# Two layers of a hybrid encoder on one core: banks and order of the output projection's first group, the place where linear attention is closed, and two elementwise operations on GpSimd

## The chip, the cores and the metric

The kernel runs on one core of a Trainium2 chip. A core has five engines with queues of their own, each working strictly in order: TensorE (PE) multiplies matrices into PSUM, VectorE (DVE) and ScalarE (ACT) do elementwise work and read PSUM, GpSimd (POOL) does elementwise work in SBUF, and SyncE (SP) issues most of the transfers. Engines wait for each other by semaphores. The accumulators live in PSUM banks of 128 partitions x 512 float32.

The metric is the device time of one execution in microseconds (us). A profile is one further execution with the hardware profiler on.

## The reference

Everything is float32. Two layers run over 256 tokens with 16 learned meta tokens in front (272 columns in all), model width 2048:

```python
proj = h @ w_in        # columns: GLA q k v gate, low-rank decay, NA q k v
y_gla = gla(...)       # bidirectional gated linear attention, 4 heads
y_na  = na(...)        # 16 heads of 2-D neighbourhood attention + meta keys
mix = concat(y_gla, y_na) @ w_out
h = layer_norm(alpha * h + mix)
h = layer_norm(alpha * h + square(relu(h @ w_ff1)) @ w_ff2)
```

The linear attention of a head ends in a norm over its 256 values and a gate:

```python
o = o * rsqrt(mean(square(o), axis=-1) + eps) * norm_w   # per head
o = o * silu(r)
```

The neighbourhood attention is a softmax of each token's scores over its window and the meta tokens; the 16 meta tokens attend among themselves, a softmax of 16 x 16 per head (kept here in a 16 x 48 tile with a mask). The meta rows are dropped from the result, so layer 1 computes the mixer's output and what follows for the 256 tokens only (n = 256; in layer 0 n = 272).

## The kernel before, in words

Activations stand transposed, features on the partitions and tokens along a row. A weight block is 128 x 1024 float32 (`raw`, loaded by SP at L195). Each block, and each activation, is split into a rounded high part and the remainder: `wh` by ScalarE (L218), `wl` by VectorE (L219). A product is then three passes (high by high, high by low, low by high), 24 matmuls of 272 columns for a block. Blocks are made two ahead, from buffers of three, so a `wl` that comes late stops TensorE.

Outputs are computed in groups of four. `by_m` goes output by output (L253, in layer 1 partly L265): an accumulator is finished over all of k before the next. `by_k` (L304, in layer 1 L314 by `dense`) holds four accumulators and goes through k in pairs; it is used where the activations become ready one by one, as for the first group of the output projection, whose inputs `y` come out of the two kinds of attention: `y[0..7]` from linear attention, `y[8..15]` from neighbourhood attention. Ahead of each k pair it calls `mixed`, which makes sure that this pair of `y` is done and adds up the residual (`acc`, L424).

PSUM has eight banks in two pools of four: `pm` (tiles `mm`: accumulators, and in this stage the scores of neighbourhood attention) and `pb` (tiles `bg`, handed out by `bank()`: everything else in the background). A bank is reused when its last reader is done.

Two queues of generators run in the background of the projections: `bg` holds the heads of linear attention one after another, `fg` the eight pairs of heads of neighbourhood attention (`na_pair`, pairs 0 to 7). `pump` lets them go on by a credit in the middle and at the end of each output. The 24 q/k/v outputs of neighbourhood attention are six groups (g = 0 to 5); pair c can begin when output 3c + 2 is there, so pair 6 begins after the first output of group 5, and pair 7 after the last. What is left of `bg` is forced ahead of group 5.

The program order of each engine's queue comes from a scheduler that follows the order of the code but may move an instruction by its own model.

The end of a head of linear attention: squares of the outputs (`grs`, `gtn`), their sum (L725), the split of the sum into `sp` (ScalarE L339, VectorE L340), two matmuls with a matrix of 1/256 that give the mean (L983), the inverse root by Newton steps (L574 to L578) and the scaling that gives two `y`.

The end of a neighbourhood pair: scores on TensorE (L778, for the meta tokens L782), bias added by VectorE (L787 to `ns`, L789 to `nms`), maximum (L754), exponentials on ScalarE (L756), reciprocals of the sums (L757), products (L760; for `ns` and its rest `npr` on GpSimd, for the meta rows `nms` on VectorE), then transposes: those of `ns` and `npr` on VectorE (L799, L800), those of the values and of `nms` on TensorE (L805 to L808). A trip through memory (`hop` to `np`) puts the turned weights in place for the products with the values (L851, L858). The values and keys of a pair stand in `nv` and `nk`, with their neighbours' columns in `nr` (L540, L541, L544).

Of the kernel before, what the change touches and what calls it, by code (L numbers as in the profile page):

```python
# [7 lines left out]
F32 = mybir.dt.float32  # L8
# [3 lines left out]
ALU = mybir.AluOpType  # L12
PSUM = bass.MemoryType.PSUM

P = 128
# [19 lines left out]
GLA_R, GLA_NA, NORMS = 1.3, 1.4, (1.0, 0.6)  # L35
# [23 lines left out]
class Trunk:  # L59
# [216 lines left out]
        self.nc.vector.tensor_tensor(t, t, parts[0], ALU.add)  # L276
        return t

    def by_k(self, acts, n, before, wide=False):

        ps = [self.pm.tile([P, 512], F32, name="mm", tag="mm") for _ in range(4)]
        if wide:
            ps += [self.bank() for _ in range(4)]
        nk = len(acts)
        for k in range(0, nk, 2):
            before(k)
            if n == T:
                self.dense(ps, acts[k:k + 2], self.weights(), k)
                continue
            for g in range(0, len(ps), 4):  # L290
                wh, wl = self.weights()
                parts = ((wh, 0), (wh, 1), (wl, 0))
                order = [(j, p, m) for j in range(2) for p in range(3) for m in range(4)]
                first = wide and not k
                if first and not g:
                    order.sort(key=lambda o: (o[0], o[2] // 2))
                elif wide and k == 2 and not g:
                    order.sort(key=lambda o: o[1])
                elif first:
                    order.sort(key=lambda o: o[1] // 2)  # L300
                else:
                    order.sort(key=lambda o: (k and o[2], o[1] // 2, o[2]))
                for j, p, m in order:
                    self.nc.tensor.matmul(ps[g + m][:, :n], lhsT=self.block(parts[p][0], 4 * j + m if first else 2 * m + j), rhs=acts[k + j][parts[p][1]][:, :n],  # L304
                                          start=k + j + p == 0, stop=k == nk - 2 and j + p == 3)
        return [[p[:, :T], p[:, T:]] if n == T else [p[:, :n]] for p in ps]
# [46 lines left out]
    def layer(self, l):  # L353
        nc, tc = self.nc, self.tc
        self.l = l
        self.full = l + 1 < DEPTH
        self.n = n = L if self.full else T
        with ExitStack() as actx:
            pool = lambda name, side, ctx=actx, bufs=1: ctx.enter_context(
                tc.tile_pool(name=name, bufs=bufs, side=side, reuse_waits="tile"))  # L360
            a = pool("att", "left")
            t = lambda nm, s: a.tile(s, F32, name=nm, tag=nm)
            self.qk = [t(f"qk{h}", [P, 2, L]) for h in range(GH)]
            for h in range(GH) if l else ():
                nc.gpsimd.memset(self.qk[h][:, 1, T:], 0.0)
            self.decay = [t(f"dec{h}", [P, 2, L]) for h in range(GH)]
            self.V = a.tile([P, 2 * GH, 2, P], F32R, name="V", tag="V")
            self.vlow = [self.pair(self.yp, "y", 12 + h).both.rearrange("p a c -> p (a c)") for h in range(GH)]
            self.VS = a.tile([80, GH * GDV], F32R, name="VS", tag="VS")
            nc.gpsimd.memset(self.VS.bitcast(F32), 0.0)  # L370
            self.y, self.gate, self.done, self.vt = [None] * DC, {}, set(), []
            if l:
                self.load_gates()
                self.by_m(self.x, [L + 2] * 4, lambda m, ps: self.fixed(self.ev_k, m, ps), pump=(1, NORMS[0]),
                          renew=True)
                first = self.by_k(self.x, L, self.normed)
                self.drain()
                self.lctx.close()
            with ExitStack() as ectx:
                self.ep = pool("early", "right", ectx)  # L380
                self.fcredit = 0
                self.fg.append(self.gates())
                if l == 0:
                    with ExitStack() as xctx:
                        self.xr = pool("xr", "right", xctx)
                        first = self.by_k(self.x, L, self.load_x, wide=True)
                    for m in range(4):
                        self.ev_k(m, first.pop(0)[0])
                for m, ps in enumerate(first):
                    self.ev_v(m, ps[0])  # L390
                self.credit, self.alone = 0, True
                self.by_m(self.x, [L] * 4, lambda m, ps: self.ev_v(4 + m, ps), pump=(1, 1, True))
                self.by_m(self.x, [n] * 4, self.ev_q, pump=(1, 1, True))
                self.drain()
            self.a2 = pool("na", "left", bufs=2)
            with ExitStack() as gctx:
                self.credit = 0
                self.g2 = pool("gla", "right", gctx, 2)
                for h in range(GH):
                    self.bg.append(self.gla_head(h))  # L400
                for g in range(2):
                    self.by_m(self.x, [n] * 4, lambda m, ps: self.ev_r(4 * g + m, ps), pump=(1, GLA_R))
                self.na_tiles()
                for g in range(6):
                    if g == 5:
                        while self.bg:
                            self.step(self.bg, 1)
                        gctx.close()
                        self.ln_open()
                    ns = [n if (4 * g + m) % 3 == 0 else L for m in range(4)]  # L410
                    self.by_m(self.x, ns, lambda m, ps: self.ev_na(4 * g + m, ps), pump=(1, GLA_NA, True))
            self.alone = False
            ps = self.by_k(self.y, n, self.mixed)
            self.drain()
        self.tail(ps)

# [163 lines left out]
    def gla_head(self, h):  # L580
        nc, n, full, g2 = self.nc, self.n, self.full, self.g2
# [95 lines left out]
        ps = self.bank()  # L677
# [24 lines left out]
        wide = lambda t, w: bass.AP(t.tensor, t.offset, [t.ap[0], [w, 2], [1, n]])  # L702
# [8 lines left out]
        rs, tn = (g2.tile([P, L], F32, name=nm, tag=nm, bufs=1)[:, :n] for nm in ("grs", "gtn"))  # L711
        for e in range(2):
            o = self.bank()[:, :n]
# [8 lines left out]
            os_.append(g2.tile([P, L], F32, name="on", tag="on")[:, :n])  # L722
            nc.vector.tensor_tensor(os_[e], o, self.gate[2 * h + e], ALU.mult)
        yield
        nc.vector.tensor_tensor(rs, rs, tn, ALU.add)  # L725
        ms = yield from self.mean(rs, GDV, pool=g2)
        self.newton(rs, ms, self.eps, tn)
        yield
# [33 lines left out]
    def na_pair(self, c, q, k, v):  # L762
        nc, b = self.nc, self.a2
# [9 lines left out]
        ps = self.spare(2)  # L773
        for t in range(2):
            for hh, hs in enumerate(heads):
                for part in heads:
                    at = NM + t * P + part.start
                    nc.tensor.matmul(ps[hh][part, t * NKEY:t * NKEY + NKEY], lhsT=q[hs, at:at + NAD], rhs=k[hs, t, :],  # L778
                                     start=True, stop=True)
        if self.full:  # L780
# [4 lines left out]
            sm = meta[:NM, :, :NK2]  # L785
# [6 lines left out]
        yield  # L792
        if self.full:
            mt = b.tile([NM, 6], F32, name="mst", tag="mst")
            self.softmax(sm, mt, 2, ((sm, sm),), nc.vector)
        yield
        turned = b.tile([P, 4, 192], F32, name="nt", tag="nb")
        out = lambda at, n: turned[:, :, at:at + 32 * n].rearrange("p j (u c) -> p u j c", c=32)
# [483 lines left out]
```

## Time and profile before

| what | us |
|---|---|
| median of three runs | 2322.85 |
| the three runs | 2322.03, 2322.85, 2323.6 |
| the profiled execution | 2323.91 |
| its span | 2322.1 |

The granted TensorE clock was 0.999 of full speed in the profiled execution. In the rows of a timeline stand the start from the beginning of the span, the duration, the engine, the line, the operation, output <- inputs, the shape, the number of instructions joined in the row, and in brackets how long the engine stood idle before it and what ended this. `PEld` is TensorE's weight load. A matmul's duration overlaps with the next one's. In rows of the groups the columns behind the bar are busy time in us, mean of one in ns, and idle time ahead of them with what ended it. In rows of one source line stand the shortest, median and longest duration in ns, and the first and last start.

### The profile page before, as it was taken

Reading aid. Unit: us, or ns where it says so; the run is one execution under the profiler, and the core shown is the slowest. Engines: PE = TensorE matmul, PEld = TensorE weight load, DVE = VectorE, ACT = ScalarE, POOL = GpSimd, SP = SyncE. Lnnn points to the kernel's source line nnn. Section 1 sums busy time; section 2 is a strip of 40 time slices with the busy share of each in tenths; the row PEclk is TensorE's granted clock in tenths of the full one; section 3 lists DMA queues with packets and bytes.
Section 4 is the critical chain, followed back from the end, with each engine's and each line's share of the span. In section 5 each row is a group of like instructions: output and inputs, shape, how many; then the busy total and the mean of one; then the engine's idle time right before and its main releaser. Section 6 shows DMA issues by size and latency. Waiting matters only on the chain.

```text
span 2322.1 us, 45272 instructions
## 1 busy us (share of the span) xinstructions
PE 2304.2 (99%) x18420; PEld 2188.9 (94%) x18420; DVE 1526.4 (66%) x2408; ACT 1223.0 (53%) x2096; POOL 155.4 (7%) x232
## 2 busy tenths in 40 slices
PE   9999999999999999999999999999999999999998
PEld 9999999999999999999999899889988888888888
DVE  5588878875544455547576788688866555666655
ACT  5666655564433344444456766655654334555443
POOL 0023210100000000000020122200100000000000
PEclk9999999999999999999999999999999999999999
DMA  8556666565555556665655556665666666667664
GB/s 259 155 164 184 199 189 177 173 181 181 182 181 178 179 181 182 180 179 178 182 173 173 173 175 209 195 187 181 198 191 196 194 191 193 192 196 218 195 195 150
DMA packets 129824, 431.65 MB, mean 186 GB/s; under 512 B 14792, under 2 KB 23496, under 8 KB 129616
## 3 DMA queue, kind: packets, MB, share of 16 engines
q1 hardware_dynamic: 127024, 421.95, 59.9%
q10 hardware_dynamic: 2592, 6.82, 0.8%
q8 instruction: 144, 2.36, 0.4%
q14 instruction: 64, 0.52, 0.1%
HBM read 420.32 MB, written 8.39 MB: 185 GB/s over the span
## 4 chain that ended last, share of the span: by engine, by line
PE 91%; DVE 5%; ACT 2%; issue 1%; DMA 1%; POOL 0%; DVEq 0%; ACTq 0%; SPq 0%
PE mm L253 53%; PE mm L265 29%; PE mm L304 4%; PE mm L314 2%; DVE wl L219 1%; PE bg L304 1%; ACT wh L218 1%; ACT ns L756 0%; DVE S L615 0%; PE bg L851 0%; PE bg L470 0%; PE bg L629 0%; DVE acc L1085 0%; POOL dec L617 0%; DMA raw<-in_wff 0%
## 5 line engine op out<-in xcount | busy, mean ns | idle before, releaser
L219 DVE TENSOR_TENSOR wl<-raw,wh 128x1024 fp32r<-128x1024 f32 (+1 forms) x770 | 935.9, 1223 | 621.8 <-ACT wh L218 518.5
L218 ACT CAST wh<-raw 128x1024 fp32r<-128x1024 f32 (+1 forms) x770 | 804.7, 1047 | 755.8 <-PE mm L253 352.6
L253 PE MATMUL mm<-x,wh 128*128 128x272 f32 (+3 forms) x4544 | 806.8, 294 | 0.0
L253 PEld LDWEIGHTS mm<-x,wh 128*128 128x128 f32 x4544 | 648.0, 188 | 15.5 <-issue 0.8
L253 PE MATMUL mm<-x,wl 128*128 128x272 f32 (+3 forms) x2432 | 520.6, 285 | 2.9 <-DVE wl L219 2.9
L253 PEld LDWEIGHTS mm<-x,wl 128*128 128x128 f32 x2432 | 391.4, 188 | 3.4 <-DVE wl L219 3.4
L253 PE MATMUL mm<-y,wh 128*128 128x272 f32 (+1 forms) x1440 | 235.0, 285 | 0.0
L253 PEld LDWEIGHTS mm<-y,wh 128*128 128x128 f32 x1440 | 199.7, 188 | 0.1
L265 PE MATMUL mm<-x,wh 128*128 128x512 f32 x832 | 193.8, 390 | 0.0
L265 PEld LDWEIGHTS mm<-x,wh 128*128 128x128 f32 x832 | 154.3, 188 | 31.0
L253 PE MATMUL mm<-u,wh 128*128 128x272 f32 (+1 forms) x1056 | 172.1, 285 | 0.0
L265 PE MATMUL mm<-y,wh 128*128 128x512 f32 x688 | 162.3, 389 | 0.0
L265 PEld LDWEIGHTS mm<-y,wh 128*128 128x128 f32 x688 | 128.7, 188 | 26.8 <-issue 0.4
L253 PE MATMUL mm<-y,wl 128*128 128x272 f32 (+1 forms) x720 | 146.5, 284 | 0.0
L253 PEld LDWEIGHTS mm<-u,wh 128*128 128x128 f32 x1056 | 146.3, 188 | 0.0
L265 PE MATMUL mm<-u,wh 128*128 128x512 f32 x496 | 118.3, 391 | 0.0
L253 PEld LDWEIGHTS mm<-y,wl 128*128 128x128 f32 x720 | 112.5, 188 | 0.0
L265 PEld LDWEIGHTS mm<-u,wh 128*128 128x128 f32 x496 | 90.9, 188 | 17.6
L253 PE MATMUL mm<-u,wl 128*128 128x272 f32 (+1 forms) x528 | 107.4, 284 | 0.0
L265 PEld LDWEIGHTS mm<-x,wl 128*128 128x128 f32 x832 | 98.5, 188 | 2.1
L265 PE MATMUL mm<-x,wl 128*128 128x256 f32 x832 | 99.0, 276 | 0.0
L265 PEld LDWEIGHTS mm<-y,wl 128*128 128x128 f32 x688 | 84.3, 188 | 2.8
(275 smaller groups left out, 2285.0 us busy)
## 6 DMA issues: line engine op xcount, KB each, us to landing
raw<-in_wff SPq DMA_DIRECT2D x512, 512.0 KB, 3.6
raw<-in_win SPq DMA_DIRECT2D x190, 512.0 KB, 4.2
raw<-in_wout SPq DMA_DIRECT2D x64, 512.0 KB, 3.9
hop<-nt ACTq DMA_DIRECT2D x16, 384.0 KB, 2.3
np<-hop SPq DMA_DIRECT2D x64, 96.0 KB, 4.1
nb<-in_nab SPq DMA_DIRECT2D x16, 352.0 KB, 4.4
xraw<-in_xT SPq DMA_DIRECT2D x7, 272.0 KB, 5.8
out<-out SPq DMA_DIRECT2D x5, 256.0 KB, 3.1
```

The lines of the kernel that those rows point to most:

```text
L218: self.nc.scalar.copy(h, r)
L219: self.wl = self.nc.vector.tensor_tensor(lo, r, h.bitcast(F32), ALU.subtract).ins
L253: mm(o, lhsT=self.block(w, j), rhs=rhs, start=first and not i, stop=last and i == len(TURNS[once]) - 1)
L265: self.nc.tensor.matmul(o, lhsT=self.block(both[j // 8][low], j % 8), rhs=rhs, start=first and not i + j, stop=bool(last and i and j == 15 ...
L304: self.nc.tensor.matmul(ps[g + m][:, :n], lhsT=self.block(parts[p][0], 4 * j + m if first else 2 * m + j), rhs=acts[k + j][parts[p][1]][:, ...
L314: self.nc.tensor.matmul(o, lhsT=self.block(both[low], i), rhs=rhs, start=not low and k + i % 2 == 0, stop=k == DC - 2 and i % 2 == 1 and n ...
```

## The change

Three things change. First, in both layers `by_k` is called with `ends=True` for the output projection's first group: two of the four accumulators come from `pb` and two from `pm`, where all four came from `pm`. With 272 columns (layer 0) the first k pair is then ordered output by output, as the later pairs are; the order of `dense` (layer 1) has no such key and stays. Second, group 5 of the neighbourhood outputs is made in two halves, and what is left of `bg` is forced between them instead of ahead of the group. Third, the sum of the squares of a head (L725, 8 times: 4 heads in 2 layers) and the normalisation of the meta softmax (`nms`, L760, 8 times, layer 0 alone) move from VectorE to GpSimd. Lines behind the first edits count one or two more: L304 is L305, L725 is L727, L760 is L762, L808 is L810, L983 is L985.

```diff
-    def by_k(self, acts, n, before, wide=False):
-
-        ps = [self.pm.tile([P, 512], F32, name="mm", tag="mm") for _ in range(4)]
+    def by_k(self, acts, n, before, wide=False, ends=False):
+
+        tile = lambda n: [self.pm.tile([P, 512], F32, name="mm", tag="mm") for _ in range(n)]
+        ps = [self.bank(), self.bank()] + tile(2) if ends else tile(4)
...
-                    order.sort(key=lambda o: (k and o[2], o[1] // 2, o[2]))
+                    order.sort(key=lambda o: ((k or ends) and o[2], o[1] // 2, o[2]))
...
                 for g in range(6):
-                    if g == 5:
-                        while self.bg:
-                            self.step(self.bg, 1)
-                        gctx.close()
-                        self.ln_open()
                     ns = [n if (4 * g + m) % 3 == 0 else L for m in range(4)]
-                    self.by_m(self.x, ns, lambda m, ps: self.ev_na(4 * g + m, ps), pump=(1, GLA_NA, True))
+                    for at in ((0, 2), (2, 4)) if g == 5 else ((0, 4),):
+                        if at == (2, 4):
+                            while self.bg:
+                                self.step(self.bg, 1)
+                            gctx.close()
+                            self.ln_open()
+                        self.by_m(self.x, ns[slice(*at)], lambda m, ps: self.ev_na(4 * g + at[0] + m, ps), pump=(1, GLA_NA, True))
             self.alone = False
-            ps = self.by_k(self.y, n, self.mixed)
+            ps = self.by_k(self.y, n, self.mixed, ends=True)
...
-        nc.vector.tensor_tensor(rs, rs, tn, ALU.add)
+        nc.gpsimd.tensor_tensor(rs, rs, tn, ALU.add)
...
-            self.softmax(sm, mt, 2, ((sm, sm),), nc.vector)
+            self.softmax(sm, mt, 2, ((sm, sm),), nc.gpsimd)
```

Where the instructions stand shows in the program order of the engines' queues (a row is a run of like instructions with the count behind x; numbers behind a name tell tiles apart). TensorE in layer 0 at the end of the last head, before (`mm<-x` are the q/k/v outputs; group 5 begins behind L983):

```order
L253 MATMUL mm<-x_622,wl 128x272
L253 MATMUL mm<-x_625,wl 128x272
L983 MATMUL bg<-sp_4524,onesr_653 128x272 x2
L253 MATMUL mm<-x_132,wh 128x272 x2
L253 MATMUL mm<-x_133,wh 128x272 x2
```

and after, at the end of group 5's first output, with the scores of pair 6 ahead of the same two matmuls:

```order
L853 MATMUL bg<-np,v_4136 64x128 x4
L853 MATMUL bg<-np,v_4135 64x128 x8
L860 MATMUL bg<-npm_2212,v_4136 64x16 x4
L780 MATMUL mm<-nk,nq 64x176 x8
L784 MATMUL mm<-nk,nq 64x48 x2
L985 MATMUL bg<-sp_4524,onesr_653 128x272 x2
L253 MATMUL mm<-x_132,wh 128x272 x2
```

The two matmuls stand one output later. TensorE at the start of layer 0's output projection, behind the scores of pair 7, before:

```order
L782 MATMUL mm<-nk,nq 64x48 x2
L304 MATMUL mm<-y_1488,wh 128x272 x2
L304 MATMUL mm<-y_1566,wh 128x272 x2
L304 MATMUL mm<-y_1488,wh 128x272 x2
L304 MATMUL mm<-y_1566,wh 128x272 x2
L304 MATMUL mm<-y_1488,wl 128x272
L304 MATMUL mm<-y_1566,wl 128x272
L304 MATMUL mm<-y_1488,wl 128x272
L304 MATMUL mm<-y_1566,wl 128x272
```

and after:

```order
L784 MATMUL mm<-nk,nq 64x48 x2
L305 MATMUL bg<-y_1488,wh 128x272 x2
L305 MATMUL bg<-y_1566,wh 128x272 x2
L305 MATMUL bg<-y_1488,wl 128x272
L305 MATMUL bg<-y_1566,wl 128x272
L305 MATMUL bg<-y_1488,wh 128x272 x2
L305 MATMUL bg<-y_1566,wh 128x272 x2
L305 MATMUL bg<-y_1488,wl 128x272
L305 MATMUL bg<-y_1566,wl 128x272
L305 MATMUL mm<-y_1488,wh 128x272 x2
```

Two accumulators are `bg` tiles now and come first, each finished for this k pair before the next. GpSimd at the last two pairs of layer 0, before:

```order
L760 TENSOR_TENSOR npr_2208<-ns,nst 128x4x48
L544 COPY nk<-nk 128x32 x2
L544 COPY nr_2206<-nv_2205 128x32 x2
L760 TENSOR_TENSOR ns<-ns,nst 128x4x128
L760 TENSOR_TENSOR npr_2210<-ns,nst 128x4x48
```

and after:

```order
L762 TENSOR_TENSOR npr_2208<-ns,nst 128x4x48
L762 TENSOR_TENSOR nms_2216<-nms_2216,mst 16x2x48
L546 COPY nk<-nk 128x32 x2
L546 COPY nr_2206<-nv_2205 128x32 x2
L762 TENSOR_TENSOR ns<-ns,nst 128x4x128
L762 TENSOR_TENSOR npr_2210<-ns,nst 128x4x48
L762 TENSOR_TENSOR nms_2218<-nms_2218,mst 16x2x48
```

The meta normalisation stands behind the other two products in GpSimd's queue.

## The prediction, made before the changed kernel ran

> **What bounds the kernel now.** I read the page first (busy shares and the chain that ended last), then TensorE's idle time by its releasers, then the timeline around each place that the change touches.
>
> ```profile
> PE 2304.2 (99%) x18420; PEld 2188.9 (94%) x18420; DVE 1526.4 (66%) x2408; ACT 1223.0 (53%) x2096; POOL 155.4 (7%) x232
> PE 91%; DVE 5%; ACT 2%; issue 1%; DMA 1%; POOL 0%; DVEq 0%; ACTq 0%; SPq 0%
> ```
>
> TensorE is busy 99% of the span and carries 91% of the chain. The change removes no matmul, so it can win only the places where TensorE stands still, and it loses whatever new stops it makes. The first place is where layer 0 empties its linear attention, ahead of the last group of q/k/v outputs:
>
> ```profile
> 303.56 0.65 PE L253 MATMUL mm<-x,wh 128*128 128x272 f32 x4
> ...
> 304.05 0.41 PE L253 MATMUL mm<-x,wl 128*128 128x272 f32 x2
> ...
> 305.59 0.87 PE L983 MATMUL bg<-sp,onesr 128*128 128x272 f32 x2 [1.13 <-ACT sp L339]
> 306.07 0.19 PEld L983 LDWEIGHTS bg<-sp,onesr 128*128 128x128 f32 x1 [0.29 <-DVE sp L340]
> ```
>
> Four matmuls start in 0.49 us (303.56 to 304.05), so one takes 0.122 us. After the two of 304.05 the next was due at 304.29 and came at 305.59: 1.30 us. The second L983 matmul came 0.48 us behind the first instead of 0.12: 0.36 us. So 1.65 us stand here; the 1.13 in brackets is 0.17 less than the true loss, since the end of a matmul is modelled. I add that 0.17 to other bracketed waits of this kind. Layer 1 has the same place:
>
> ```profile
> 1483.70 0.41 PE L253 MATMUL mm<-x,wl 128*128 128x272 f32 x2
> ...
> 1485.08 0.84 PE L983 MATMUL bg<-sp,onesr 128*128 128x256 f32 x2 [0.97 <-ACT sp L339]
> ```
>
> Due at 1483.94, started at 1485.08: 1.14 us. The two matmuls then take 0.84 instead of about 0.5: together 1.5 us. The other places are the starts of the two output projections. Layer 0:
>
> ```profile
> 335.38 0.77 PE L304 MATMUL mm<-y,wh 128*128 128x272 f32 x4 [0.83 <-DVE nr L541]
> 337.48 0.74 PE L304 MATMUL mm<-y,wh 128*128 128x272 f32 x4 [0.83 <-DVE nms L789]
> 337.81 0.88 DVE L754 TENSOR_REDUCE nst<-ns 128x4 f32<-128x704 f32 x1
> 338.94 1.05 ACT L218 CAST wh<-raw 128x1024 fp32r<-128x1024 f32 x1 [2.34 <-PE mm L304]
> 339.89 0.44 ACT L756 ACTIVATE ns<-ns,nst 128x176 f32<-128x176 f32 x1
> 341.16 0.78 DVE L424 TENSOR_TENSOR acc<-x 128x272 f32<-128x272 f32 x2
> 341.87 0.17 DVE L757 RECIPROCAL nst<-nst 128x4 f32<-128x4 f32 x1
> 342.19 1.04 POOL L760 TENSOR_TENSOR ns<-ns,nst 128x512 f32<-128x512 f32 x1 [6.74 <-DVE nst L757]
> 342.56 0.78 DVE L760 TENSOR_TENSOR nms<-nms,mst 16x96 f32<-16x96 f32 x1
> 343.18 0.52 POOL L760 TENSOR_TENSOR npr<-ns,nst 128x192 f32<-128x192 f32 x1
> 343.48 0.30 PE L808 MATMUL bg<-ident,nms 128*128 128x128 f32 x1 [0.70 <-DVE nms L760]
> ```
>
> Three waits with 0.17 each added: 1.0, 1.0 and 0.87, together 2.85 us. The first two wait for banks: an accumulator's bank still holds a q/k/v output (nr) or the scores of the last pair (nms L789). The third waits for the softmax of that pair. Layer 1 has one such wait:
>
> ```profile
> 1514.10 1.96 PE L314 MATMUL mm<-y,wh 128*128 128x512 f32 x6 [0.89 <-DVE nr L541]
> ```
>
> That is 1.06 us, and some 0.2 more inside the row for the scores' bank: 1.25. All that the change aims at is 1.65 + 1.5 + 2.85 + 1.25 = 7.25 us, 0.31% of the span.
>
> **The change, part by part.** *Linear attention closed two outputs later.* In the new order the two L983 matmuls stand behind the output matmuls and the scores of pair 6, some 50 matmuls (6 us) later. Their input sp was there 1.3 us late, so it is early by over 4 us: −1.65 and −1.5 us. What was forced ahead of the group (square root, Newton steps, scaling, splits of y6 and y7) now falls beside pair 6's softmax on VectorE and ScalarE:
>
> ```profile
> 319.26 0.18 DVE L757 RECIPROCAL nst<-nst 128x4 f32<-128x4 f32 x1 [1.80 <-ACT ns L756]
> ...
> 321.72 1.17 DVE L219 TENSOR_TENSOR wl<-raw,wh 128x1024 fp32r<-128x1024 f32 x1
> ...
> 323.75 0.41 PE L253 MATMUL mm<-x,wl 128*128 128x272 f32 x2
> ```
>
> That wl ends at 322.89 and is used at 323.75: slack 0.86 us. About 3 us of VectorE work comes in ahead of it, into an idle stretch of 1.80 us before the reciprocal and about 1 us behind it. I take 0 us, with 0 to 1 for the range.
>
> *Output projection, layer 0.* Two accumulators move to the other pool, whose banks are free by then; output by output, the third falls on the bank that waits for nothing now, and the fourth is reached after its nr. Both bank waits go: −2.0 us. The third place is late next. Without those waits TensorE reaches it at about 343.48 − 0.87 − 2.0 = 340.6 and must still have the meta scores normalised. That chain moves only partly: the scores' reduction ends at 338.69 whatever TensorE does; ScalarE's weight copy of 338.94, which waited for TensorE, comes before it, so the exponentials start near 338.9 instead of 339.89. The reciprocal falls near 340.9, GpSimd's ns ends near 342.1 and npr near 342.65. Now the change puts nms behind these two on GpSimd, where VectorE had it beside them. The price of such an operation on GpSimd:
>
> ```profile
> L760 POOL TENSOR_TENSOR npr<-ns,nst 128x192 f32<-128x192 f32 x16 | 9.4, 590 | 0.0
> L617 POOL TENSOR_TENSOR dec<-dec 128x272 f32<-128x272 f32 x8 | 6.0, 754 | 126.4 <-DVE S L615 126.4
> L617 POOL TENSOR_TENSOR dec<-dec 128x68 f32<-128x68 f32 x8 | 4.3, 543 | 10.5 <-DVE S L615 10.5
> L617 POOL TENSOR_TENSOR dec<-dec 128x4 f32<-128x4 f32 x8 | 2.6, 325 | 15.2 <-DVE S L615 15.2
> ...
> L760 DVE TENSOR_TENSOR nms<-nms,mst x8: 203/204/775, 200.9 to 342.6; 16x96 f32<-16x96 f32 x8
> ```
>
> For 96 elements I take 0.5 us, between 0.33 (4 elements) and 0.59 (192). nms is then ready at 343.15 and the matmul starts near 343.25, where it stood at 343.48; with a matmul or two of other work fewer ahead of it, the net is −0.35 us of the 2.85. The bounds: −1.25 if nms costs nothing more than VectorE's, +0.9 if it is held for a whole wl (1.22).
>
> The other seven pairs of layer 0 (layer 1 has no meta rows) pay where the matmul follows closely:
>
> ```profile
> 216.57 0.70 POOL L760 TENSOR_TENSOR npr<-ns,nst 128x192 f32<-128x192 f32 x1
> 217.27 0.27 PE L808 MATMUL bg<-ident,nms 128*128 128x128 f32 x1
> ...
> 231.44 0.51 POOL L760 TENSOR_TENSOR npr<-ns,nst 128x192 f32<-128x192 f32 x1
> 232.50 0.30 PE L808 MATMUL bg<-ident,nms 128*128 128x128 f32 x1
> ...
> 298.83 0.15 DVE L757 RECIPROCAL mst<-mst 16x2 f32<-16x2 f32 x1 [0.33 <-ACT nms L756]
> 299.42 0.29 PE L808 MATMUL bg<-ident,nms 128*128 128x128 f32 x1
> ```
>
> Pair 1: npr ends at 217.27, the very start of the matmul, so 0.5 and the 0.1 that lies between the end of nms (343.34) and L808 (343.48) above: +0.6. Pair 2: 231.95 + 0.6 against 232.50: +0.05. Pair 5: 298.98 + 0.6 against 299.42: +0.15. The other four leave 1.2 us or more by my reading of the same rows there. Sum +0.8, bounds +0.3 and +1.4. The Trainium skill (GPSIMD Reference, 4.1 Engine selection) keeps two-input elementwise work on VectorE, GpSimd being about twice as slow; by that estimate nms would cost 0.41 us and this sum 0.5. The rows here say 1.8 times (0.754 against 0.41 for the same width) and more for small tiles.
>
> *Output projection, layer 1.* Its order stays; the output that waits for nr is now the fourth instead of the second, reached about 1 us later: 1.25 falls to about 0.25, so −1.0 (0 to −1.25).
>
> *The norm's add on GpSimd,* 8 of them, 0.75 instead of 0.41 us. One had TensorE waiting at another place:
>
> ```profile
> 1328.79 0.41 DVE L725 TENSOR_TENSOR grs<-grs,gtn 128x256 f32<-128x256 f32 x1
> ...
> 1329.69 0.38 PE L983 MATMUL bg<-sp,onesr 128*128 128x256 f32 x1 [1.22 <-ACT sp L339]
> ```
>
> GpSimd need not queue behind VectorE there, and ends 0 to 0.4 us earlier; I take −0.1. The rest hide: before the group's last outputs sp had no TensorE waiting, and at the two closings it is now early.
>
> The sum: −1.65 − 0.35 + 0.8 in layer 0, −1.5 − 1.0 − 0.1 in layer 1: −3.8 us. The profiled execution took 2323.91 us, so 2320.1; the median of the three runs is 1.06 us lower (2322.85), so 2319.05. I forecast 2319.1, that is −0.16%. A difference under 0.2% (4.65 us) can't be told from none here.
>
> **The rivals.** *All of it goes through.* If the last pair's softmax of layer 0 also comes early enough (nms −1.25 instead of −0.35), the other pairs cost 0.3 and layer 1 gains its full 1.25: −5.5 or more, up to −7.0 us, 2316 to 2317.4. For it: every wait named is in the rows. Against it: the reduction's end at 338.69 does not depend on what the change touches.
>
> *No net gain.* The waits return at pair 6 (a wl late by 1 us in each layer) and at nms: 0 to −1 us, 2322 to 2323. For it: slack of only 0.86 us there; against it: the idle 1.80 us that the added work can fill.
>
> *GpSimd is held up, and TensorE with it: slower.* A GpSimd operation that starts beside a wl ends with it:
>
> ```profile
> 277.08 1.41 POOL L617 TENSOR_TENSOR dec<-dec 128x8 f32<-128x8 f32 x1 [1.21 <-DVE S L615]
> 277.20 1.21 DVE L219 TENSOR_TENSOR wl<-raw,wh 128x1024 fp32r<-128x1024 f32 x1
> ...
> L617 POOL TENSOR_TENSOR dec<-dec x56: 216/462/2857, 108.7 to 1458.1; 128x272 f32<-128x272 f32 x8, 128x136 f32<-128x136 f32 x8, 128x68 f32<-128x68 f32 x8, 128x34 f32<-128x34 f32 x8
> ```
>
> 1.41 us where the median is 0.46, and the longest 2.86. Each nms held 2.86 us would cost TensorE 2.9, 2.4 and 2.5 us at pairs 1, 2 and 5, 1.7 at pair 4 and 2.0 at pair 7: 11.5, against gains of 4.6, so +7 us, 2330. Held by one wl each (1.7 us) it is +5.5 − 4.6: about +1, 2324. It passes 0.2% from a mean hold of about 2.4 us. Against it: at pairs 2, 5 and 7 the next wl stands behind this softmax's last VectorE work, so nms starts first. The Trainium skill (SBUF — State Buffer, Who interferes with whom) says that a VectorE instruction with two SBUF inputs and a GpSimd one that reads SBUF exclude each other for a whole instruction, the first to start winning. The two rows agree, and by that rule wl waits 0.5 us for nms oftener than the reverse, which has slack.
>
> **How the numbers follow.** The forecast (−2 to −4.6 us) has 0.45, all of it 0.32, no net gain 0.12, GpSimd held 0.11 (most of that beyond one wl each). Faster by over 0.2%: 0.32; within: 0.57; slower: 0.11. The range runs from 2316.2 (nearly the whole 7 us) to 2323.8 (no gain, with a us of scatter in the runs); below it and above it lie about 0.2.
>
> **What would show it.** L983 of heads 3 without a wait at both closings; the starts of both output projections without waits for banks in layer 0 and one short one in layer 1; one longer wait, 2.5 to 3 us, at the last pair's nms, now named after GpSimd; 0.5 us at pair 1. I am wrong if that wait at nms is short (then 2317), if wl L219 shows up as a releaser near pair 6, or if nms on GpSimd takes over a microsecond.

## The result and the profile after

Over 15 runs each, run side by side, the changed kernel took 2319.42 us (median; 2317.1 to 2320.7) and the kernel before 2323.03 us (2321.48 to 2326.37): a ratio of 0.9982, with a 95% interval of 0.9975 to 0.9989. A second set of 11 runs of the changed kernel gave 2319.31 us and 0.998 (0.9971 to 0.9989). That is 3.6 us less by the medians; the first interval allows 0.11% to 0.25%, so a gain is shown, but not on which side of 0.2% it lies. The forecast was 2319.1 us.

The profiled execution after took 2318.1 us with a span of 2316.3 us, 5.8 us less than the profiled execution before. By the starts of like matmuls in the two traces, about 0.9 us of that lies in the first 77 us, where nothing was changed, and 0.5 us in the last 360, so these two profiles overstate the gain; the waits below account for 4.0 us.

The page's first row after:

```profile
PE 2301.6 (99%) x18420; PEld 2188.1 (94%) x18420; DVE 1520.9 (66%) x2392; ACT 1224.7 (53%) x2096; POOL 160.8 (7%) x248
```

The same number of matmuls, 16 operations fewer on VectorE and 16 more on GpSimd. What TensorE waited for, before and then after (engine, line, what it waited for: us in total, times, longest):

```profile
PE bg L983 <- ACT sp L339: 3.3, 3, 1.2
PE mm L253 <- DVE wl L219: 2.9, 2, 2.3
...
PE mm L314 <- DVE nr L541: 0.9, 1, 0.9
PE mm L304 <- DVE nr L541: 0.8, 1, 0.8
PE mm L304 <- DVE nms L789: 0.8, 1, 0.8
PE bg L808 <- DVE nms L760: 0.7, 1, 0.7
```

```profile
PE bg L810 <- POOL nms L762: 2.8, 2, 2.4
PE mm L253 <- DVE wl L219: 2.1, 1, 2.1
...
PE bg L985 <- ACT sp L340: 0.8, 1, 0.8
...
PE bg L853 <- DVE v L814: 0.5, 1, 0.5
PE mm L315 <- DVE nr L543: 0.2, 1, 0.2
```

Two of the three waits for sp went, both waits for banks in layer 0 went, and the one in layer 1 shrank. Against that the wait for nms grew from 0.7 to 2.4 us (and a second one of 0.3 us appeared), and a wait for v is new. One of the two waits for wl went as well. The timeline after shows the three new waits, the chain behind the longest, and the two matmuls of the last head's mean:

```profile
216.82 0.33 PE L810 MATMUL bg<-ident,nms 128*128 128x128 f32 x1 [0.34 <-POOL nms L762]
...
310.79 0.52 PE L985 MATMUL bg<-sp,onesr 128*128 128x272 f32 x2
...
338.10 0.16 DVE L759 RECIPROCAL nst<-nst 128x4 f32<-128x4 f32 x1
338.41 1.04 POOL L762 TENSOR_TENSOR ns<-ns,nst 128x512 f32<-128x512 f32 x1 [5.46 <-DVE nst L759]
339.40 0.51 POOL L762 TENSOR_TENSOR npr<-ns,nst 128x192 f32<-128x192 f32 x1
339.87 0.34 POOL L762 TENSOR_TENSOR nms<-nms,mst 16x96 f32<-16x96 f32 x1
340.26 0.33 PE L810 MATMUL bg<-ident,nms 128*128 128x128 f32 x1 [2.42 <-POOL nms L762]
...
1517.43 0.87 PE L853 MATMUL bg<-np,v 64*64 64x128 f32 x20 [0.55 <-DVE v L814]
```

The two matmuls of the last head's mean (310.79) now start without a wait. The last pair's meta scores come out of GpSimd as the third of three products, and TensorE stands for 2.4 us until then.

For comparison across kernels I use the loss at a place: the distance between two matmul starts, less the usual distance of that shape in the same trace (0.122 us for 272 columns, 0.109 us for a transposition). It counts the part of a wait that the brackets leave out. In us:

| place | before | after | banks only | closing only | GpSimd only | add only |
|---|---|---|---|---|---|---|
| layer 0, linear attention closed (sp) | 1.65 | 0 | 1.64 | 0 | 0.63 | 0.78 |
| layer 0, output projection, banks | 1.98 | 0 | 0 | 2.51 | 1.56 | 1.66 |
| layer 0, last pair's nms | 0.87 | 2.59 | 1.83 | 0.87 | 1.42 | 0.87 |
| layer 0, pair 1's nms | 0 | 0.51 | 0 | 0 | 0.51 | 0 |
| layer 0, wl near 278 us | 0.79 | 0 | 0.77 | 0.77 | 0 | 0.59 |
| layer 1, first head (sp) | 1.39 | 1.36 | 1.50 | 1.41 | 1.37 | 1.07 |
| layer 1, linear attention closed (sp) | 1.49 | 0 | 1.50 | 0 | 0.91 | 0.92 |
| layer 1, output projection, banks | 1.26 | 0.33 | 0 | 1.88 | 1.10 | 1.15 |
| layer 1, values of the last pair (v) | 0 | 0.81 | 0.75 | 0 | 0 | 0 |
| sum | 9.43 | 5.60 | 7.99 | 7.44 | 7.50 | 7.04 |

The sum falls by 3.8 us from before to after; the wait for wl near 1457 us (2.48 before, 2.27 after), which no part touches, makes it 4.0. (That wait lies between 2.2 and 2.8 us over all traces of this study.)

### The profile page after: what moved, and what is told of

Its sections match the earlier page's. It is cut to its first block, busy times and chain, and to the rows that moved or that the text cites. A ratio compares the mean times of both kernels' runs of the same rounds, so it can differ in the third digit from the quotient of the medians.

```text
span 2316.3 us, 45253 instructions
## 1 busy us (share of the span) xinstructions
PE 2301.6 (99%) x18420; PEld 2188.1 (94%) x18420; DVE 1520.9 (66%) x2392; ACT 1224.7 (53%) x2096; POOL 160.8 (7%) x248
## 4 chain that ended last, share of the span: by engine, by line
PE 80%; DVE 2%; ACT 1%; issue 1%; POOL 0%; DMA 0%; DVEq 0%; ACTq 0%; SPq 0%; POOLq 0%
PE mm L253 44%; PE mm L265 30%; PE mm L305 2%; PE mm L315 1%; DVE wl L219 1%; PE bg L315 0%; ACT wh L218 0%; PE bg L305 0%; DVE acc L1087 0%; PE bg L853 0%; DVE S L617 0%; ACT ns L758 0%; PE bg L985 0%; PE bg L472 0%; DMA raw<-in_win 0%
```

## The experiments

All were timed in five rounds beside the kernel before.

**Only the banks and the order.** The changed kernel with the closing and both GpSimd operations as before:

```diff
-                    for at in ((0, 2), (2, 4)) if g == 5 else ((0, 4),):
...
+                    if g == 5:
+                        while self.bg:
+                            self.step(self.bg, 1)
+                        gctx.close()
+                        self.ln_open()
...
-        nc.gpsimd.tensor_tensor(rs, rs, tn, ALU.add)
+        nc.vector.tensor_tensor(rs, rs, tn, ALU.add)
...
-            self.softmax(sm, mt, 2, ((sm, sm),), nc.gpsimd)
+            self.softmax(sm, mt, 2, ((sm, sm),), nc.vector)
```

> Only the banks and the order of the output projection's first group are changed. My theory: in layer 0 the two bank waits at its start go (-2.0 us), but TensorE then stands at the last pair's meta scores, whose chain hardly moves; with the normalisation on VectorE that wait is about 1.9 us where it was 0.87, so -1.0 net. In layer 1 the wait for nr goes from 1.06 + 0.2 to 0.3 (-0.9) and 0.8 us comes back later at L853, where the values' bank of the last pair is now needed again too soon. Sum -1 us. Rival (all of the gain from the banks stays): -3 us or more.

Measured: 2321.88 us against 2323.93, ratio 0.9987 (0.9979 to 0.9996). In layer 0 both bank waits went and the loss at nms rose from 0.87 to 1.83: of 1.98 us, 1.0 was kept. In layer 1, 1.26 went and 0.75 came back at the values. The losses of the table fall by 1.4 us; the time alone, with an interval of 0.9 to 4.9 us, can't decide between the theory and the rival. Its rows in the list of TensorE's waits:

```profile
PE bg L809 <- ACT wh L218: 1.7, 1, 1.7
...
PE bg L852 <- DVE v L813: 0.5, 1, 0.5
```

I read the first row as the wait for the meta scores under another name: the matmul's input is nms, and a wait for several semaphores is put down to the one that came last by the records. In the three traces in which this wait is named after VectorE's nms (before, closing only, add only), the matmul starts 0.14 us after nms ends (343.34 and 343.48 before). Here it does so too: nms ends at 342.36, the matmul starts at 342.50. The theory holds: the banks free TensorE, and the softmax behind them then holds it.

**Only the closing two outputs later.**

```diff
-            ps = self.by_k(self.y, n, self.mixed, ends=True)
+            ps = self.by_k(self.y, n, self.mixed)
...
-        nc.gpsimd.tensor_tensor(rs, rs, tn, ALU.add)
+        nc.vector.tensor_tensor(rs, rs, tn, ALU.add)
...
-            self.softmax(sm, mt, 2, ((sm, sm),), nc.gpsimd)
+            self.softmax(sm, mt, 2, ((sm, sm),), nc.vector)
```

> Only the closing of linear attention is moved by two outputs. My theory: the waits before L983 (L985 here) of the last head go in both layers, -1.65 and -1.5 us, nothing else changes: -3.1 us, most of what the whole change gains. Rival (the work forced there is needed and its delay comes back as a late wl at pair 6 or later): -1 us or less, with a new wait for wl near pair 6.

Measured: 2321.66 us against 2323.93, ratio 0.999 (0.9981 to 0.9999). Both closings lost their waits, and no wl came late at pair 6, so the rival falls. But the expectation of 3.1 us was too high (the losses of the table fall by 2.0 us): at the starts of the output projections the bank waits grew, 0.5 us in layer 0 and 0.6 us in layer 1. Row of its timeline:

```profile
332.42 1.23 DVE L219 TENSOR_TENSOR wl<-raw,wh 128x1024 fp32r<-128x1024 f32 x1 [1.21 <-ACT wh L218]
333.56 0.18 DVE L543 COPY nr<-mm 128x32 f32<-128x32 f32 x1
333.80 0.77 PE L305 MATMUL mm<-y,wh 128*128 128x272 f32 x4 [1.36 <-DVE nr L543]
```

The copy that frees the bank stands behind a wl in VectorE's queue, and did not come forward as much as TensorE did: 0.83 us idle before, 1.36 here. So a part of what the closing wins is kept only because the accumulators take other banks.

**Only the two operations on GpSimd.**

```diff
-            ps = self.by_k(self.y, n, self.mixed, ends=True)
+            ps = self.by_k(self.y, n, self.mixed)
...
-                    for at in ((0, 2), (2, 4)) if g == 5 else ((0, 4),):
...
+                    if g == 5:
+                        while self.bg:
+                            self.step(self.bg, 1)
```

> Only the two small operations are on GpSimd. My theory: 0.5 us lost at pair 1's nms in layer 0, about 0.7 us lost at the last pair's nms (the wait of 0.87 grows to 1.5), and 0.8 us won at the wl of 278 us if taking the 0.2 us operation off VectorE is what removed that wait; the add changes nothing that TensorE sees. Sum about +0.4 us. Rival (VectorE is relieved and gains in general): -1 us or more.

Measured: 2322.19 us against 2323.93, ratio 0.9994 (0.9985 to 1.0002), so the time alone tells little. The losses do: pair 1 and the last pair paid 0.51 and 0.55 us as expected, and the wait at 278 us went as expected. Not expected: the closings improved by 1.0 and 0.6 us without being moved. The timeline at layer 0's closing, first before and then in this run:

```profile
303.95 0.79 DVE L723 TENSOR_TENSOR on<-bg,gate 128x272 f32<-128x272 f32 x2
304.66 0.43 DVE L725 TENSOR_TENSOR grs<-grs,gtn 128x272 f32<-128x272 f32 x1
```

```profile
302.58 1.15 POOL L726 TENSOR_TENSOR grs<-grs,gtn 128x272 f32<-128x272 f32 x1 [3.50 <-ACT gtn L722]
303.59 0.79 DVE L724 TENSOR_TENSOR on<-bg,gate 128x272 f32<-128x272 f32 x2
303.75 0.42 ACT L340 CAST sp<-grs 128x272 fp32r<-128x272 f32 x1 [1.25 <-POOL grs L726]
304.23 0.39 PE L984 MATMUL bg<-sp,onesr 128*128 128x272 f32 x1
304.78 0.39 PE L984 MATMUL bg<-sp,onesr 128*128 128x272 f32 x1 [0.16 <-DVE sp L341]
```

On VectorE the add stood behind the products of line 723 and ran at 304.66; on GpSimd it took 1.15 us instead of 0.43 and was still done sooner, at 303.73 against 305.09. TensorE itself was 0.26 us ahead here (the mean's first matmul was due at 304.03, and at 304.29 before), so 1.1 us of that is the add's own: it began 0.08 us after ScalarE's second square (gtn) was done at 302.50.

**Only the add on GpSimd**, to tell the two operations apart: as the run before, with nms on VectorE.

```diff
-            self.softmax(sm, mt, 2, ((sm, sm),), nc.gpsimd)
+            self.softmax(sm, mt, 2, ((sm, sm),), nc.vector)
```

> Only the norm's add is on GpSimd; closing, banks and nms as before. My theory: at the two places where linear attention is closed the add no longer stands behind VectorE's queue, so the waits before the means' matmuls (1.65 and 1.5 us) fall to about 0.4 and 0.9, as with both GpSimd edits: -1.8 us there; nms and the wait of 0.8 us for wl near 278 us stay. Rival (taking nms off VectorE is what brought those waits down): the two waits stay at 1.65 and 1.5 us.

Measured: 2321.9 us against 2323.99, ratio 0.9991 (0.9982 to 1.0). The closings lost 0.78 and 0.92 us, where they had lost 1.65 and 1.49; the wait at 278 us stayed with 0.59. So the add brings the closings' gain, and nms most of the gain at 278 us. The closings' 0.78 was 0.4 more than expected, in two parts (0.35 at the first matmul, 0.43 at the second). A further wait stands in this trace alone, 0.91 us at 1237 us for a copy by ScalarE (ft L506); the table leaves it out, and its cause was not looked for.

**The changed kernel with nms back on VectorE.**

```diff
-            self.softmax(sm, mt, 2, ((sm, sm),), nc.gpsimd)
+            self.softmax(sm, mt, 2, ((sm, sm),), nc.vector)
```

> The whole change, but nms stays on VectorE. My theory: the wait at the last pair's nms falls from 2.6 to about 1.9 us, the 0.5 us at pair 1 go, and the wait for wl near 278 us (0.8 us) comes back: -0.4 us against the changed kernel. Rival (the wait for wl went for another reason, or by chance): it stays away, and -1.2 us.

Measured: 2318.3 us against 2323.93, ratio 0.9976 (0.9966 to 0.9986); the interval overlaps that of the changed kernel, so the two can't be told apart by time. The loss at the last pair was 2.17 and 0.25 directly behind it, hardly less than 2.59, where about 1.9 was expected:

```profile
339.20 1.04 POOL L762 TENSOR_TENSOR ns<-ns,nst 128x512 f32<-128x512 f32 x1 [5.46 <-DVE nst L759]
339.68 0.67 DVE L762 TENSOR_TENSOR nms<-nms,mst 16x96 f32<-16x96 f32 x1
340.49 0.45 PE L810 MATMUL bg<-ident,nms 128*128 128x128 f32 x1 [2.00 <-ACT wh L218]
```

On VectorE nms did not run freely beside GpSimd's ns. In all five traces with the last pair's nms on VectorE it starts while ns runs, takes 0.65 to 0.78 us where the median before is 0.204, and ends 0.11 us after ns (here 340.35 and 340.24). On GpSimd, behind ns and npr, it ends 0.76 us after ns. So the move to GpSimd makes this chain 0.65 us longer, less than npr and nms together. The wait itself shows 0.42 of it (2.17 against 2.59): here ns starts 0.15 us later against TensorE, and the matmul follows VectorE's nms after 0.14 us, where it follows GpSimd's after 0.05.

Pair 1 lost nothing, and near 278 us the wait was back. The rows of the changed kernel, then of this one:

```profile
274.36 0.71 DVE L801 STREAM_TRANSPOSE nt<-ns 128x512 f32<-128x512 f32 x1 [0.54 <-POOL ns L762]
...
275.85 0.27 POOL L619 TENSOR_TENSOR dec<-dec 128x8 f32<-128x8 f32 x1 [0.76 <-DVE S L617]
275.96 1.24 DVE L219 TENSOR_TENSOR wl<-raw,wh 128x1024 fp32r<-128x1024 f32 x1
```

```profile
275.03 0.71 DVE L801 STREAM_TRANSPOSE nt<-ns 128x512 f32<-128x512 f32 x1 [0.55 <-POOL ns L762]
...
275.67 0.21 DVE L762 TENSOR_TENSOR nms<-nms,mst 16x96 f32<-16x96 f32 x1
...
276.68 1.41 POOL L619 TENSOR_TENSOR dec<-dec 128x8 f32<-128x8 f32 x1 [1.22 <-DVE S L617]
276.80 1.21 DVE L219 TENSOR_TENSOR wl<-raw,wh 128x1024 fp32r<-128x1024 f32 x1
...
278.06 0.52 PE L253 MATMUL mm<-x,wl 128*128 128x272 f32 x2 [0.44 <-DVE wl L219]
```

In all eight traces of this study with nms on GpSimd at that pair the loss at this place is 0.24 us or less; in the five with nms on VectorE (before, banks, closing, add only, this one) it is 0.59 to 0.79. This one nms of 0.2 us is not the whole cause. TensorE is 0.30 us later here than in the changed kernel (its matmuls of 275.26 start at 275.56), but VectorE's transposition ahead of nms is 0.67 us later, and the wl behind it 0.84. So against TensorE, VectorE has lost 0.37 us by the time nms starts, and 0.54 by the wl. The 0.37 was gathered earlier. The same comparison gives 0.03 us just ahead of pair 1's stop and 0.59 behind it, where TensorE no longer stops for 0.51 us; then about 0.13 more at each of the next two nms, and 0.5 less at a wl near 256 us. Taken together, pair 1 and this wl lose 0.60 us in this kernel and 0.51 + 0.09 in the changed one (the table writes 0 for the 0.09).

**The changed kernel with the add back on VectorE.**

```diff
-        nc.gpsimd.tensor_tensor(rs, rs, tn, ALU.add)
+        nc.vector.tensor_tensor(rs, rs, tn, ALU.add)
```

> The changed kernel with the norm's add back on VectorE. Theory: where closing is late the add's place does not matter, so both closings stay without a wait; 0 to +0.4 us at the first head of layer 1 (wait 1.35 now). Rival (the add is what takes the closings' waits away): up to 3 us of waits come back before the means' matmuls.

Measured: 2319.37 us against 2323.36, ratio 0.9981 (0.9972 to 0.999), the changed kernel's own. No wait at either closing; 1.13 us at the first head of layer 1 (1.36 with the add on GpSimd), so there the expected 0 to +0.4 had the wrong sign. So with the late closing the add's place no longer matters. The add and the closing are two ways to win the same wait, and their gains don't add: the losses of the three parts fall by 1.4, 2.0 and 1.9 us alone, 5.4 together, and by 3.8 us in the whole.

**The changed kernel once more**, beside the next runs.

> The changed kernel again, beside the runs of this group. Both theories: about 3.6 us faster than before; TensorE's waits as in its first profile, 9 us in all.

Measured: 2319.31 us, as given above; the same waits; the losses above 0.25 us make 9.5 us over the whole trace (9.0 in the first). The largest difference was at layer 1's bank: 0.63 here, 0.33 there.

**The last pair's values in the accumulators' pool.** In the new kernel two banks of `pb` are taken by accumulators, and two of `pm` stand empty behind the scores of the last pair.

```diff
-        pv = self.bank()
+        pv = self.pm.tile([P, 512], F32, name="mm", tag="mm") if c == 7 else self.bank()
```

> The changed kernel, but the last pair's values are transposed into a bank of the accumulators' pool, two of whose banks are free then. My theory: in layer 1 the new wait of 0.8 us for v before the products with the values goes, all else as in the changed kernel: -0.8 us. Rival (those products are held by the copy itself or by a later transfer): the wait stays or moves behind.

Measured: 2318.36 us against 2323.99, ratio 0.9975 (0.9965 to 0.9985). The wait for v went, and 0.55 us came at the next products with the values, which wait for their transfer:

```profile
1517.60 0.89 PE L853 MATMUL bg<-np,v 64*64 64x128 f32 x24
...
1524.57 0.87 PE L853 MATMUL bg<-np,v 64*64 64x128 f32 x12 [0.39 <-DMA np<-hop]
```

So the bank was the cause of the wait for v, but two thirds of it moved behind: the rival had that part right. The bank wait at the start of this projection was 0.91 us here. Over the eight traces with the new banks and the late closing it lies between 0.33 and 1.06; what sets it was not tested. In time this run can't be told from the changed kernel.

**The last pair's meta scores turned later, first try.** Built on the run before. All pairs' fourth transposition moved into a function, called behind the copies of the values, and for the last pair one k pair later (2.9 us of TensorE work):

```diff
-        if self.full:
-            nc.tensor.transpose(pv[:, T + P:], meta.rearrange("p u c -> p (u c)"), self.ident)
...
+        def turn():
+            nc.tensor.transpose(pv[:, T + P:], meta.rearrange("p u c -> p (u c)"), self.ident)
+            for hh, hs in enumerate(heads):
+                nc.vector.tensor_copy(pm[hs, hh, :], pv[hs, T + P:T + P + NM])
+
+        if self.full and c < 7:
+            turn()
```

> As the run before, and the transposition of the last pair's meta scores (nms) stands one k pair, about 2.9 us of TensorE work, later. My theory: the wait of 2.6 us for nms goes, but the transfer of that pair's weights (hop to np), which waits for the same softmax, comes late at the pair's products with the values instead, so a wait of 1 to 1.6 us appears there: -1 to -1.6 us against the run before. Rival (nms alone holds TensorE): -2.6 us.

Measured: 2326.3 us against 2323.99, ratio 1.0009 (1.0 to 1.0018). Both theories missed, because the edit did something else too: at every pair of layer 0 the transposition now writes into a bank behind the copies out of that bank. It lost 0.2 to 2.1 us at each of the eight pairs:

```profile
PE bg L816 <- DVE v L812: 4.1, 3, 1.9
...
PE bg L816 <- DVE Am L645: 1.8, 1, 1.8
...
PE bg L816 <- DVE near L647: 1.1, 1, 1.1
...
PE mm L816 <- DVE v L812: 0.8, 1, 0.8
```

At four pairs the wait is named after the copy of v out of that bank, at two after other work of VectorE. Against the run before it is 7.9 us more for a few lines moved, and it says nothing on the question.

**The same, mended.** The first seven pairs keep their order; the last pair's meta scores get a bank of their own. The values' bank stays in the accumulators' pool; the expectation calls that run e6.

```diff
-        if self.full:
+        late = self.full and c == 7
+        if self.full and not late:
             nc.tensor.transpose(pv[:, T + P:], meta.rearrange("p u c -> p (u c)"), self.ident)
...
-            for hh, hs in enumerate(heads):
+            for hh, hs in enumerate(heads if not late else ()):
...
         if c == 7:
+            if late:
+                mv = self.pm.tile([P, 512], F32, name="mm", tag="mm")
+                nc.tensor.transpose(mv[:, :P], meta.rearrange("p u c -> p (u c)"), self.ident)
+                for hh, hs in enumerate(heads):
+                    nc.vector.tensor_copy(pm[hs, hh, :], mv[hs, :NM])
             self.due.popleft()()
```

> The late transposition of nms mended: the other seven pairs keep their order, and the last pair's meta scores get a bank of their own, one k pair later. My theory: the wait of 2.5 us for nms goes and 1 to 1.6 us come back at that pair's products with the values, whose transfer (np) waits for the same softmax: -1 to -1.6 us against e6. Rival (nms alone holds TensorE): -2.5 us.

Measured: 2316.13 us against 2323.36, ratio 0.997 (0.9958 to 0.9981).

```profile
340.51 0.34 POOL L762 TENSOR_TENSOR nms<-nms,mst 16x96 f32<-16x96 f32 x1
...
340.98 0.27 PE L837 MATMUL mm<-ident,nms 128*128 128x128 f32 x1
...
343.98 1.75 SPq L829 DMA_DIRECT2D np<-hop  x4
...
348.17 1.31 PE L859 MATMUL bg<-np,v 64*64 64x128 f32 x17
```

nms is ready at 340.85 and its matmul starts at 340.98 without a wait; the products with the values start at 348.17 and lose 0.37 us on the way, where the theory had 1 to 1.6. So by the trace the rival is nearer: of 2.5 us, 2.1 stay won at these places, and the transfer np had more slack than I took it to have. The times don't decide it: each against its own runs of the kernel before, this one gains 7.2 us and e6 5.6, a difference of 1.6, and the intervals overlap.

**The same, with pair 1's nms on VectorE.**

```diff
-            self.softmax(sm, mt, 2, ((sm, sm),), nc.gpsimd)
+            self.softmax(sm, mt, 2, ((sm, sm),), nc.vector if c == 1 else nc.gpsimd)
```

> As the run before, with pair 1's nms on VectorE. Theory: the 0.5 us at pair 1 go and nothing else moves, -0.5 us. Rival (VectorE, a little later, holds the next wl or state there): 0 or a new wait near 217 to 222 us.

Measured: 2316.01 us (5 runs, 2314.53 to 2316.78) against 2323.36, ratio 0.9967 (0.9954 to 0.9979). The wait at pair 1 went, and 0.24 us stand at the wl near 278 us, where the run before lost 0.09:

```profile
277.38 0.30 PEld L253 LDWEIGHTS mm<-x,wl 128*128 128x128 f32 x2 [0.29 <-DVE wl L219]
277.38 0.52 PE L253 MATMUL mm<-x,wl 128*128 128x272 f32 x2
```

So a part of what nms on GpSimd wins near 278 us hangs on the stop at pair 1: VectorE gains on TensorE while TensorE stands. The expectation that nothing else moves was wrong by this 0.15 us. In time the run can't be told from the run before. It has the lowest median of the study, 0.33% below the kernel before; its interval only just overlaps that of the changed kernel's first set (0.9975 to 0.9989).

## Why the prediction was right

The forecast of 2319.1 us stood 0.3 us from the median, and the sum of its steps (3.8 us) is that of the losses in the table; the interval of the time itself (2.6 to 5.8 us) is much wider than this agreement. Step by step:

- *Linear attention closed later, −1.65 and −1.5 us.* Measured exactly so. Newton's steps beside pair 6's softmax cost nothing, and no wl came late there. Not foreseen: alone it would have given back 1.1 us at the banks, which the first part of the change takes away.
- *Output projection, layer 0, −0.35 of 2.85 us.* Measured −0.26: the bank waits went, and the loss at nms became 2.59. The argument that the softmax moves only partly was right, and the mended late transposition shows that this wait alone held TensorE for 2.1 of the 2.5 us. One premise was wrong: before, VectorE did not have nms beside GpSimd's products. It ended 0.11 us after ns (343.34 and 343.23). So nms back on VectorE gave 2.42 us instead of 2.59, and not the whole difference between −0.35 and −1.25.
- *nms on GpSimd.* I took 0.5 us; eight operations took:

```profile
L762 POOL TENSOR_TENSOR nms<-nms,mst x8: 335/336/533, 199.2 to 339.9; 16x96 f32<-16x96 f32 x8
```

  0.336 us, at the low end of my bounds. So pair 1 paid 0.51 (0.6 forecast) and pairs 2 and 5 nothing (0.2 forecast): +0.5 for +0.8. The prediction expected small tiles to be relatively slower on GpSimd than the add; the ratio to VectorE was 1.65 for nms (336 and 204 ns) and 1.84 for the add.
- *Output projection, layer 1, −1.0 us.* The loss went from 1.26 to 0.33 (0.63 in the second trace): −0.9 and −0.6.
- *The first head of layer 1, −0.1 us.* Measured −0.03.
- *Two terms that I did not have.* I counted the banks only at the start of the projection. With two banks of `pb` held to its end, the last pair's values and its products compete for the other two, and layer 1 lost 0.81 us at L853. And I gave VectorE's relief no price, where the wait of 0.79 us near 278 us went, in part because TensorE had stopped at pair 1 instead. The two cancel, so part of the closeness is luck.
- *The rival of GpSimd held up* did not come: the longest nms took 0.533 us, the adds 0.736 to 1.208 us. The two rows at 277 us that the prediction reads as agreeing with its rule agree only in part: the two operations did not run freely side by side, but the first to start did not win. The dec there started 0.12 us before the wl, took 1.41 us and ended after it, while the wl took its usual 1.21. In the changed kernel dec started 0.11 us before the same wl and took 0.27. The rival in which all goes through needed an early nms, and this was the step that failed it. "No net gain" fell with the closings.

The chances put 0.57 on a change within 0.2%; the measured 0.18% lies there, close to the edge. That a difference under 0.2% can't be told from none was too careful: both intervals of the changed kernel stay below 1.

## What to carry to other kernels

A wait that a change removes uncovers the next one on the same engine: price the chain that TensorE reaches next, not the wait by itself. Two edits that remove the same wait do not add, and an edit may hold its gain only through another one; each part alone and one part taken back show which. Where a wait is a matter of order, placing the waiting instruction behind work that is there anyway (here a k pair) took 2.1 us off the losses, where having the awaited operation on the quicker engine took 0.2. The traces show this; the times are too close to show it.

## What the runs showed that was not expected

An operation that takes nearly twice as long on GpSimd (0.776 us median against 0.422 for the add) can still finish 1.1 us sooner there, because it does not stand in VectorE's queue. VectorE's nms of 0.2 us took 0.65 to 0.78 us wherever it started while GpSimd's ns ran (the last pair in five traces), and ended 0.11 us after ns each time. And a stop of TensorE is not only lost: while it stood 0.5 us at pair 1, VectorE gained on it, and a later wait for wl was shorter by 0.15 us.
